# Product one of a seven-product block is copied into a kept PSUM bank, and product two is added onto it by TensorE

## The chip, the cores and the metric

The kernel runs on one core of one Trainium2 chip. The metric is the device time of one execution in microseconds (us). Before the change three runs took 914.67, 915.05 and 915.2 us, so the median is 915.05 us.

## The reference

The reference is a trunk of two layers over one sequence of 256 tokens with 1024 features, all in float32. Each layer has a feed-forward part, a mixer and a second feed-forward part, and each part is followed by a layer norm over a scaled residual:

```python
def swiglu(x, w_in, w_out):
    gu = x @ w_in
    g, u = gu[..., :D_FF], gu[..., D_FF:]
    return (jax.nn.silu(g) * u) @ w_out
...
        x = layer_norm(ALPHA * x + 0.5 * swiglu(x, ffn_w_in[l, 0], ffn_w_out[l, 0]), ln_g[l, 0], ln_b[l, 0])
...
        x = layer_norm(ALPHA * x + y, ln_g[l, 1], ln_b[l, 1])
        x = layer_norm(ALPHA * x + 0.5 * swiglu(x, ffn_w_in[l, 1], ffn_w_out[l, 1]), ln_g[l, 2], ln_b[l, 2])
```

`y` is the mixer's output: a bidirectional mLSTM in the first layer, windowed attention with grouped queries in the second. `D_FF` is 2816. In the kernel this makes six stages: FFN, mLSTM, FFN, FFN, attention, FFN. The change touches the code of the four FFN stages alone, but the order of the work changes in all six.

## The kernel before

Every large product is made in a split form. An operand is written as a high part and a low part in a reduced format, and `mm3` (line 625) does three matmuls for one: high by high, high by low, low by high. A weight tile of 128x1024 is loaded by a DMA into a raw buffer (`w_raw`, `s_raw`). ScalarE casts it to `w_hi` and VectorE subtracts to get `w_lo`. There are ten buffers for each of these two.

An FFN stage works through its 2816 hidden columns in five parts (`PARTS`): two blocks of seven products, a unit, and two more blocks of seven products. A unit is a plain gate and up product for 256 columns. A block, `seven` (line 883), makes 512 hidden columns for two halves of 128 tokens by a Strassen-like scheme: seven products of 128 tokens by 512 columns over half the depth take the place of eight. Some weights of these products are sums of weight tiles. They are formed in the raw buffers, by VectorE (`s_raw<-s_raw,s_raw`) or by a DMA from GpSimd's queue that adds onto a raw buffer. So such a raw buffer is used, added onto, cast again, and used again.

The seven products of a block follow one another in the order 1, 2, 5, 6, 7, 3, 4 of the functions that run behind them: `end1`, `end2`, `end5`, `end6`, `end7`, `end3`, `end4`. Each product is twelve matmuls of 128x512 into one PSUM bank. `qa` takes product one, and later takes others that are added onto what it holds. `qc` takes product two, and `qb` takes product five and later product three. The gate of the first token half is product one plus product two. Before the change `end1` copies `qa` to a buffer `t` in SBUF (ScalarE, `COPY t<-p`), `end2` adds `qc` to it (VectorE, `TENSOR_TENSOR t<-t,p`), and `end6` applies silu in place (ScalarE, `ACTIVATE t<-t`). `end3` is the last to read `qb`. Between the products stand transposes of earlier results (`p<-ident,t`, with `ident` the identity) and pieces of the output product (`down`), whose four banks stay in use through the stage. There are eight PSUM banks in all, shown as `p_88` to `p_95` in the order of the instructions.

What sets the order of all work is a list of numbers. Nothing is issued while the program is described. Every call on an engine is recorded (line 327), and `issue` (line 308) replays the records in the order of the list `ORDER`. A second list, `SLOTS`, says which buffer each request for a tile gets, PSUM banks included. So all instructions on engines and queues carry the line 317 of `issue` in the profile, and they are told apart by their tiles. Each engine takes its own instructions strictly in that order, and waits on semaphores for what it needs from another.

Of the kernel before, what the change touches and what calls it, by code (L numbers as in the profile page):

```python
# [11 lines left out]
AF = mybir.ActivationFunctionType  # L12
# [252 lines left out]
        "365018925167"),  # L265
    "t.0": ("10423251205145435305135232350"),
    "stats": ("101001110110"),
    "mv": ("011010011101"),
    "rs": ("100011011011"),
    "raw.1": ("12301301302312032103102130302130"),  # L270
    "wt.1": ("3210"),
# [1215 lines left out]
```

## Time and profile before

| | before |
|---|---|
| median of three runs | 915.05 us |
| profiled execution, span | 914.3 us |
| PE matmuls | 903.8 us busy, 99%, 4382 of them |
| PE weight loads (PEld) | 748.2 us, 82% |
| VectorE (DVE) | 812.8 us, 89%, 987 instructions |
| ScalarE (ACT) | 576.8 us, 63%, 796 instructions |
| GpSimd (POOL) | 156.8 us, 17% |
| granted TensorE clock | 0.998 |
| memory traffic | 208.52 MB, mean 228 GB/s |

The span of the profiled execution is the time from the first to the last instruction in its trace. It lies 0.75 us below the median of the timed runs. The busy share of an engine is an average over the whole program. PE's share counts a matmul from its start to its end, and successive matmuls overlap, so that a short loss between two of them shows in their start times and not in the share.

### The profile page before, as it was taken

How to read it: one execution, taken by the hardware profiler on the slowest of the kernel's cores; microseconds unless marked ns; L12 is line 12 of the kernel's file. 1: busy time of each engine (PE TensorE's matmuls, PEld its weight loads, DVE VectorE, ACT ScalarE, POOL GpSimd, SP SyncE). 2: the span in 40 equal slices, each digit the busy share in tenths (PEclk: the TensorE clock that was granted, in tenths of full speed). 3: DMA queues.
4: the chain of work that ended last, by engine and by line, in shares of the span. 5: the costliest groups of instructions: out<-in, count | busy, mean ns of one | idle time of the engine just before them, and what ended most of it. 6: DMA issues, size and time to landing. Idle time of an engine off the chain costs nothing.

```text
span 914.3 us, 12376 instructions
## 1 busy us (share of the span) xinstructions
PE 903.8 (99%) x4382; PEld 748.2 (82%) x4382; DVE 812.8 (89%) x987; ACT 576.8 (63%) x796; POOL 156.8 (17%) x200
## 2 busy tenths in 40 slices
PE   9999999999999999999999999999999999999996
PEld 7888888889988888887888888888887788888885
DVE  6998989997798999888999988899899899988897
ACT  6667567557655677565747666666488557666560
POOL 0211112113311121111012111120435311202110
PEclk9999999999999999999999999999999999999999
DMA  9999889558273889898957899987543396997971
GB/s 334 299 298 298 246 248 240 180 179 263 94 260 114 270 252 256 269 280 197 341 196 188 229 277 296 277 178 259 173 173 116 116 277 166 257 303 174 321 182 46
DMA packets 100670, 208.52 MB, mean 228 GB/s; under 512 B 6872, under 2 KB 21232, under 8 KB 100608
## 3 DMA queue, kind: packets, MB, share of 16 engines
q1 hardware_dynamic: 82832, 173.83, 54.1%
q0 software_dynamic: 17632, 33.64, 22.4%
q8 instruction: 34, 0.56, 0.2%
q10 hardware_dynamic: 144, 0.26, 0.1%
q14 instruction: 28, 0.23, 0.1%
HBM read 206.65 MB, written 1.05 MB: 227 GB/s over the span
## 4 chain that ended last, share of the span: by engine, by line
PE 96%; DMA 2%; DVE 1%; issue 1%; ACT 0%; DVEq 0%; POOL 0%; POOLq 0%
PE p L317 96%; DMA s_raw<-in_ffn_w_in_dram 1%; DMA ln_g<-in_ln_g_dram 1%; DVE w_lo L317 0%; DVE x L317 0%; ACT w_hi L317 0%; DVE h_lor L317 0%; DVEq L1483 0%; DVE hc_lor L317 0%; DVE t L317 0%; ACT xT_hi L317 0%; DVE stats L317 0%; DVE mv L317 0%; POOL ji L317 0%; DVE ident L317 0%
## 5 line engine op out<-in xcount | busy, mean ns | idle before, releaser
L317 ACT CAST w_hi<-s_raw 128x1024 fp32r<-128x1024 f32 x239 | 244.5, 1051 | 94.5 <-PE p L317 56.4
L317 DVE TENSOR_TENSOR w_lo<-s_raw,w_hi 128x1024 fp32r<-128x1024 f32 x239 | 285.6, 1218 | 19.6 <-ACT w_hi L317 15.6
L317 ACT CAST w_hi<-w_raw 128x1024 fp32r<-128x1024 f32 (+1 forms) x167 | 172.1, 1041 | 77.9 <-PE p L317 37.6
L317 DVE TENSOR_TENSOR w_lo<-w_raw,w_hi 128x1024 fp32r<-128x1024 f32 (+1 forms) x167 | 199.8, 1208 | 14.5 <-ACT w_hi L317 13.3
L317 PE MATMUL p<-w_hi,xT_hi 128*128 128x512 f32 x512 | 191.9, 394 | 0.8 <-ACT w_hi L317 0.5
L317 PE MATMUL p<-w_lo,xT_hi 128*128 128x512 f32 x512 | 192.1, 394 | 0.0
L317 PE MATMUL p<-w_hi,xT_lo 128*128 128x512 f32 x512 | 191.3, 394 | 0.0
L317 PE MATMUL p<-w_hi,h_lor 128*128 128x512 f32 (+1 forms) x323 | 119.9, 390 | 0.1
L317 PE MATMUL p<-w_hi,h_hir 128*128 128x512 f32 (+1 forms) x323 | 119.5, 391 | 0.0
L317 PE MATMUL p<-w_lo,h_hir 128*128 128x512 f32 (+1 forms) x323 | 118.6, 389 | 0.0
L317 PEld LDWEIGHTS p<-w_hi,xT_hi 128*128 128x128 f32 x512 | 95.8, 188 | 20.4 <-ACT w_hi L317 1.0
L317 PEld LDWEIGHTS p<-w_lo,xT_hi 128*128 128x128 f32 x512 | 96.0, 188 | 19.5 <-DVE w_lo L317 0.4
L317 PEld LDWEIGHTS p<-w_hi,xT_lo 128*128 128x128 f32 x512 | 96.1, 188 | 19.3 <-DVE xT_lo L317 0.3
L317 POOL DMA_DIRECT2D s_raw<-in_ffn_w_in_dram x43 | 52.2, 1266 | 329.0 <-DVE w_lo L317 90.5
L317 PE MATMUL p<-w_hi,S_hir 128*128 128x512 f32 x256 | 96.9, 390 | 0.0
L317 PE MATMUL p<-w_hi,S_lor 128*128 128x512 f32 x256 | 96.8, 390 | 0.0
L317 PE MATMUL p<-w_lo,S_hir 128*128 128x512 f32 x256 | 96.8, 390 | 0.0
L317 PEld LDWEIGHTS p<-w_hi,h_lor 128*128 128x128 f32 x323 | 60.6, 188 | 12.6 <-DVE h_lor L317 0.5
L317 PEld LDWEIGHTS p<-w_lo,h_hir 128*128 128x128 f32 x323 | 60.7, 188 | 12.2
L317 PEld LDWEIGHTS p<-w_hi,h_hir 128*128 128x128 f32 x323 | 60.5, 188 | 12.3 <-ACT h_hir L317 0.2
L317 PEld LDWEIGHTS p<-w_hi,S_hir 128*128 128x128 f32 x256 | 48.0, 188 | 10.5 <-ACT t L317 0.4
L317 PEld LDWEIGHTS p<-w_lo,S_hir 128*128 128x128 f32 x256 | 48.1, 188 | 10.1 <-DVE w_lo L317 0.2
(187 smaller groups left out, 1176.7 us busy)
## 6 DMA issues: line engine op xcount, KB each, us to landing
s_raw<-in_ffn_w_in_dram SPq DMA_DIRECT2D x101, 512.0 KB, 6.0
w_raw<-in_ffn_w_in_dram SPq DMA_DIRECT2D x58, 512.0 KB, 6.3
s_raw<-in_ffn_w_out_dram SPq DMA_DIRECT2D x55, 512.0 KB, 5.8
s_raw<-in_ffn_w_in_dram POOLq DMA_DIRECT2D x43, 512.0 KB, 7.1
w_raw<-in_ffn_w_out_dram SPq DMA_DIRECT2D x33, 512.0 KB, 7.1
w_raw<-in_ml_w_in_dram SPq DMA_DIRECT2D x24, 512.0 KB, 5.2
w_raw<-in_ffn_w_in_dram POOLq DMA_DIRECT2D x21, 512.0 KB, 7.8
s_raw<-in_ffn_w_in_dram SPq DMA_DIRECT2D x20, 256.0 KB, 6.1
```

The source lines that it names most:

```text
L317: f(*args, **kw)
```

## The change

In the second, third and fourth block of every FFN stage `qc` is no fresh bank. It is the bank `qb` of the block before, which is kept from there (`kept`). In these twelve blocks `end1` is a ScalarE copy from the bank `qa` into the kept bank. Product two starts without clearing the bank (`not seed` is the start flag, and it stands for the flag `onto` too), so TensorE adds it onto the copied product one. `end2` then applies silu straight from the bank. The addition on VectorE is gone there. In the first block of a stage nothing is kept, and the copy and the addition remain. Silu moves from `end6` to `end2` in all sixteen blocks.

```diff
+            kept = []
+
             def seven(downs, turns):
...
-                qa, qc = wbank(), wbank()
+                qa = wbank()
+                qc = kept.pop() if kept else None
+                seed = qc is not None
+                qc = qc if seed else wbank()
 
                 def end1():
-                    v["g0"] = copied(qa, "e1")
+                    if seed:
+                        nc.scalar.copy(qc, qa)
+                    else:
+                        v["g0"] = copied(qa, "e1")
 
                 def end2():
-                    nc.vector.tensor_add(v["g0"], v["g0"], qc)
+                    if seed:
+                        v["g0"] = temp("g0")
+                        nc.scalar.activation(v["g0"], qc, AF.Silu)
+                    else:
+                        nc.vector.tensor_add(v["g0"], v["g0"], qc)
+                        nc.scalar.activation(v["g0"], v["g0"], AF.Silu)
...
                 def end6():
                     v["u0"] = copied(qa, "e2")
-                    nc.scalar.activation(v["g0"], v["g0"], AF.Silu)
...
                 product(qa, of(0, 0), True, end1)
                 for f in turns:
                     f()
-                product(qc, of(4, 0), True, end2)
+                product(qc, of(4, 0), not seed, end2)
                 down(downs[0])
                 qb = wbank()
+                kept.append(qb)
```

The lists `ORDER` and `SLOTS` are new throughout. The first line of `ORDER`, out of 218 before and 197 after:

```diff
-    "0 10 -9 8 2 -9 11 -10 11 15 1 -26 11 1 -11 12 1 -12 13 12 -24 13 1 11 -10 1 1 1 1 1 8 -7 17 -37 28 10 1 72 "
...
+    "0 10 -9 8 2 1 -10 11 1 1 -12 13 392 -391 1 394 -393 -12 13 1 1 -18 1 406 -405 113 -111 15 384 -383 1 112 "
...
```

The number of matmuls is 4382 before and after, with the same shapes. VectorE has 12 instructions of 128x512 fewer. ScalarE has as many as before: 12 copies go to a bank and no longer to SBUF, and 12 of 16 silus read a bank and no longer SBUF. The loads are the same.

Three places show how the new lists move the work. The first is PE around products one and two of the second block of the first stage. Before, product one goes to `p_92` and product two to `p_88`; the matmuls of both are mixed with each other, with pieces of the output product (right operand `h_...`) and with product five (`S_...`):

```order
L317 MATMUL p_92<-w_lo_83,xT_hi 128x512
L317 MATMUL p_95<-ident,t_5_157 128x128 x4
L317 MATMUL p_88<-w_lo_85,xT_hi 128x512
L317 MATMUL p_91<-w_hi_69,S_hir_0_158 128x512
L317 MATMUL p_93<-w_lo_78,h_hir_1_99 128x512
L317 MATMUL p_88<-w_hi_76,xT_lo 128x512
L317 MATMUL p_92<-w_hi_70,xT_lo 128x512
L317 MATMUL p_88<-w_hi_76,xT_hi 128x512
L317 MATMUL p_90<-w_hi_71,h_hir_1_99 128x512
```

After, product one goes to `p_93` and product two to the kept bank `p_94`:

```order
L276 MATMUL p_93<-w_lo_85,xT_hi 128x512
L276 MATMUL p_93<-w_hi_75,xT_lo 128x512
L276 MATMUL p_89<-ident,t_3_155 128x128 x4
L276 MATMUL p_91<-w_hi_76,h_hir_1_99 128x512
L276 MATMUL p_91<-w_lo_86,h_hir_1_99 128x512
L276 MATMUL p_91<-w_hi_76,h_lor_1_101 128x512
L276 MATMUL p_90<-w_hi_76,h_hir_1_99 128x512
L276 MATMUL p_94<-w_hi_77,xT_hi 128x512
L276 MATMUL p_94<-w_lo_87,xT_hi 128x512
```

Product two now begins only behind the last matmul of product one, with four transposes and four other matmuls between them. In the twelve blocks there are always four transposes there, and beside them two other matmuls of 128x512 once, three four times, four six times and five once.

The second place is ScalarE at the same block. Before, the copy of product one stands among casts of weights, and the silu of its sum follows thirteen rows later:

```order
L317 CAST h_hir_1_99<-p_95 128x4x128
L317 CAST w_hi_70<-s_raw_6_108 128x1024
L317 COPY t_5_157<-p_92 128x512
L317 CAST w_hi_74<-w_raw_65 128x1024
L317 CAST w_hi_69<-s_raw_7_109 128x1024
```

After, the copy goes into the kept bank:

```order
L276 ACTIVATE t_2_154<-p_92 128x512
L276 CAST w_hi_68<-s_raw_7_109 128x1024
L276 COPY p_94<-p_93 128x512
L276 CAST h_hir_1_99<-p_89 128x4x128
L276 CAST w_hi_70<-w_raw_65 128x1024
```

The cast right ahead of the copy needs a raw buffer onto which VectorE has added another. In nine of the twelve blocks the instruction ahead of the copy is such a cast; in two it is a cast of a buffer that was only loaded, and in one a cast that waits for neither.

The third place is PE in the attention stage, where the scores are made (left operand `kk`, 64 rows; right operand `q2r`). Before, six such matmuls stand together, and other products separate them from the next six:

```order
L317 MATMUL p_90<-kk_hir_0_227,q2r_0_238 128x256
L317 MATMUL p_91<-kk_hir_0_227,q2r_0_238 128x256
L317 MATMUL p_92<-xT_hi,w_hi_71 128x256
L317 MATMUL p_94<-xT_hi,w_lo_83 128x256
L317 MATMUL p_92<-xT_lo,w_hi_71 128x256
...
L317 MATMUL p_92<-xT_lo,w_hi_76 128x256
L317 MATMUL p_90<-kk_hir_0_227,q2r_0_238 128x256
L317 MATMUL p_90<-kk_lor_0_228,q2r_0_238 128x256
```

After, twelve stand together:

```order
L276 MATMUL p_89<-xT_lo,w_hi_74 128x256
L276 MATMUL p_89<-xT_hi,w_lo_78 128x256
L276 MATMUL p_90<-kk_hir_0_227,q2r_0_238 128x256
L276 MATMUL p_91<-kk_hir_0_227,q2r_0_238 128x256
L276 MATMUL p_90<-kk_lor_0_228,q2r_0_238 128x256
...
L276 MATMUL p_91<-kk_hir_0_227,q2r_0_238 128x256
L276 MATMUL p_93<-xT_hi,w_hi_77 128x256
```

The 96 score matmuls stood in 18 such groups and now stand in 12. Over the whole program PE changed between kinds of matmul (512 columns, transposes, 256 columns, scores) so that there were 396 runs of one kind, and there are now 203.

More of the change, by code (lines that the diff above doesn't have):

```diff
@@ L39 @@
 ORDER = (
[208 rows of a table removed]
[187 rows of a table added]
 )
 SLOTS = {
-    "raw.0": ("210375894260ab315798a1b2380476593806142893750a61b4735a0286b12a940280"),
-    "p": ("3015273416371651624740737037743003470071732475045321703262751465120457615023462034756305172461503713"
-        "6442055504252022042555024574651034561742340220420324423044423643153426021762340152301647420765314722"
-        "060227602276670206205326743621306753342132312243113214236"),
-    "h_hir.0": ("01001"),
-    "h_lor.0": ("10101"),
-    "w_hi": ("1536089427819056375820935612483172106249564780132954061782549302675180974325916874210359678241306597"
-        "8240637195824063718459026378591430268719546372150862437689061249085367241903758623104975268413908217"
-        "5469870321659748031256784901375628147093568273041695371208346897520134659782013465920871649356809217"
-        "5368049215063874921506387491206537891234706592318672398160257386541934670253891457260389415762058963"
-        "905268715496"),
@@ L261 @@
-    "w_lo": ("8138121742486951046580796125370164658235182350986541234970895268317504678250734095386210549378012564"
-        "3185206793418250671824930568271469351690561739512805381576130867846245869374921053769842501271093864"
-        "2053149782160345781269073541976208452176048318292137523486914603568274168732498103528769175083257419"
-        "2653801479153869204715368940125739846550169834160253046821795345869732804613859740863742798750286574"
-        "365018925167"),
-    "t.0": ("10423251205145435305135232350"),
@@ L267 @@
[L267 to L271, printed above, removed]
-    "a_hir.1": ("1010"),
-    "a_lor.1": ("0101"),
-    "den.1": ("1000"),
-    "hst.1": ("1111"),
-    "hmv.1": ("0110"),
-    "hrs.1": ("1010"),
-    "h_hir.2": ("0111001001"),
-    "h_lor.2": ("1010110101"),
-    "raw.2": ("8974561237058a96142b96a485712380b57326451983b70a26890ab75124a736b74912386b504896312b50a736271085b4a8"
-        "10954573b16809a2546289310a5b06741329"),
@@ L282 @@
-    "t.2": ("0522403125023501514432433105224023511145331025223353143455"),
-    "sc.4": ("4245315103514231504321"),
-    "raw.4": ("14301534402132530145"),
-    "nm.4": ("22010202"),
-    "sm.4": ("10221202"),
-    "pr0_hir.4": ("00100110"),
-    "pr0_lor.4": ("11101011"),
-    "pr1_hir.4": ("10010010"),
-    "pr1_lor.4": ("11000000"),
-    "o.4": ("00001101"),
+    "raw.0": ("012435869074ab12356ab2180456739a5034678a20519b34679a5b401368ab127408"),
+    "p": ("0123547602456132076151416155161415165413620547162303754162705461270450631274167023541326720651347021"
+        "5161215512161516251634730124657034241432443231343241365721435064713256470132406756023451202677072607"
+        "026762062706273453124607513642623244232624234"),
@@ new lines @@
+    "w_hi": ("0124356789102453678910245367918024356179802435761809432576180943257618940325761894037256180937425681"
+        "0937425681097342568109347265180937426518093472651893074261583907426158390476215394761392457832160947"
+        "5208149365074928136507492186350749218635097428613509742861350974862135074869215304678921504637892150"
+        "4679328150769428513706928543170692584371069258437169025843716923508462791358064729135806247158390624"
+        "715839062471"),
+    "w_lo": ("0123456789013254678901325467908132547069813254670981253467098125346709158234670915826347095182364790"
+        "5182364790512836479051832647095182364709518326470918523640791852364079185264307185264370852940761352"
+        "8409632178053249617805324697180532469718025346971802534697180253694718025369471805623947180562394718"
+        "5023649781503294786510394728651039472856103947285613094728561397408261537498062153749806521798430652"
+        "179843065127"),
@@ L292 @@
+    "t.0": ("02043104543524105203413521405"),
+    "raw.1": ("13032103210132013021031202313021"),
+    "wt.1": ("2031"),
+    "a_lor.1": ("1010"),
+    "raw.2": ("465798031627495ab834075698a3b1249a871630b9245a71264185a7093259a6b1706423b80a142b73680a5978346ba05129"
+        "6ab1840956732ab184263a971b809a547106"),
+    "t.2": ("5123540213154320530414253510441324503142154301524053141524"),
+    "sc.4": ("1240305412034521035412"),
+    "raw.4": ("23405142052301054432"),
     "h_hir.5": ("10101"),
-    "h_lor.5": ("10110"),
@@ L294 @@
-    "raw.5": ("301302356a48159237091238b9ba560b79a208614b557a9328069b1a37a14a542813"),
-    "t.5": ("22311504210332350204153145144"),
+    "raw.5": ("1321030249536a78b10268a7931b0425918b37460129a358b72a8563194b5a71063b"),
+    "t.5": ("41104253141024350452123042150"),
 }
```

393 rows, old and new, of the table ORDER are left out of this document.

## The prediction

> **What bounds the kernel now.** I read the page first: the share of each engine, then the chain that ended last.
>
> ```profile
> span 914.3 us, 12376 instructions
> PE 903.8 (99%) x4382; PEld 748.2 (82%) x4382; DVE 812.8 (89%) x987; ACT 576.8 (63%) x796; POOL 156.8 (17%) x200
> PE 96%; DMA 2%; DVE 1%; issue 1%; ACT 0%; DVEq 0%; POOL 0%; POOLq 0%
> ```
>
> TensorE is busy for 903.8 of 914.3 us and makes 96% of the chain. VectorE, though 89% busy, holds 1% of it. So work taken from VectorE is not time taken from the end; it is worth only what it takes out of PE's losses. The chain in order of time shows where these lie:
>
> ```profile
> 1.71 4.11 PE p L317 x18
> 5.84 0.58 ACT xT_hi L317
> 6.43 0.53 ACT w_hi L317
> 7.00 395.75 PE p L317 x1945
> ...
> 406.25 7.01 DMA s_raw<-in_ffn_w_in_dram
> ...
> 414.50 1.22 DVE w_lo L317
> 415.72 0.60 DVE t L317
> ...
> 416.97 10.74 PE p L317 x49
> ...
> 430.73 232.36 PE p L317 x1065
> ...
> 670.07 236.55 PE p L317 x1186
> 906.62 0.02 issue
> 906.64 0.43 DVE x L317
> ```
>
> PE runs in four long pieces. The start until 7.00 and the tail from 906.64 are chains of their own. Between them the chain leaves PE near 415, 430 and 670. The losses there are read from PE's starts, where two matmuls of 128x512 follow each other at a steady pace:
>
> ```profile
> 322.08 0.39 PE L317 MATMUL p<-w_lo,h_hir 128*128 128x512 f32 x1
> 322.30 0.39 PE L317 MATMUL p<-w_hi,h_lor 128*128 128x512 f32 x1
> ...
> 415.27 0.84 PE L317 MATMUL p<-w_lo,hc_hir 128*128 128x512 f32 x3
> 416.37 0.50 PE L317 MATMUL p<-w_hi,xT_hi 128*128 128x512 f32 x1 [0.26 <-DVE t L317]
> 416.97 0.50 PE L317 MATMUL p<-w_hi,hc_lor 128*128 128x512 f32 x1
> ...
> 430.29 0.39 PE L317 MATMUL p<-w_hi,S_hir 128*128 128x512 f32 x1
> 430.73 0.50 PE L317 MATMUL p<-w_hi,h_lor 128*128 128x512 f32 x1
> 431.07 0.39 PE L317 MATMUL p<-w_hi,h_hir 128*128 128x512 f32 x1
> ```
>
> The pace is 0.22 to 0.23 us from start to start (322.08, 322.30), though one lasts 0.39: its own end comes 0.39 after its start. At 415 the third matmul of the first row starts at 415.27 + 0.84 - 0.39 = 415.72, the next at 416.37 and the next at 416.97. Those two steps are 0.65 and 0.60, so 0.80 us is lost. At 430 two steps of 0.44 and 0.34 lose 0.33. That is **1.1 us** at two places. Everywhere else in the FFN stages PE is dense, as the busy time by stretches shows (the columns after the length are sum or PE, PEld, DVE, ACT, POOL, then clock, DMA share and GB/s):
>
> ```profile
> 10.00:170.00 160.00, 160.00 (x730) 132.08 (x729) 148.10 (x150) 109.56 (x130) 20.51 (x18) 1.00 0.94 277
> 400.00:440.00 40.00, 39.59 (x175) 31.33 (x174) 35.73 (x35) 24.43 (x30) 4.79 (x4) 1.00 0.85 234
> 440.00:640.00 200.00, 200.00 (x915) 164.63 (x914) 183.10 (x195) 127.20 (x153) 25.18 (x21) 1.00 0.84 247
> ```
>
> With PE filled for 160.00 of 160.00 us there is little to win there, and any new wait is a loss.
>
> **The change part by part.** The groups that it touches:
>
> ```profile
> L317 DVE TENSOR_TENSOR t<-t,p x56: 413/679/691, 13.5 to 885.4; 128x512 f32<-128x512 f32 x48, 128x256 f32<-128x256 f32 x8
> L317 ACT COPY t<-p x52: 565/587/595, 8.5 to 880.0; 128x512 f32<-128x512 f32 x52
> L317 ACT ACTIVATE t<-p x32: 371/592/600, 25.6 to 894.9; 128x512 f32<-128x512 f32 x24, 128x256 f32<-128x256 f32 x8
> L317 ACT ACTIVATE t<-t x16: 622/626/637, 50.0 to 880.4; 128x512 f32<-128x512 f32 x16
> ```
>
> *VectorE.* Twelve additions of 0.679 us leave: 12 x 0.679 = 8.1 us of its 812.8. They lie beside PE, so I count 0. The same 1.1 us at 415 and 430 is all they could release, and the list decides that as well; it is counted below, once.
>
> *ScalarE.* Twelve silus read a bank in place of SBUF: 12 x (0.592 - 0.626) = -0.4 us. Twelve copies write a bank in place of SBUF. No row shows a write of ScalarE to a bank. The nearest row is the copy that reads one, 0.587; for a bank at both ends I take the same, with 0.45 and 0.75 as bounds (a quarter either way; at 0.75 only the shortest of the places below would lose, 0.07). ScalarE is 63% busy, so the sum on it is hidden: 0.
>
> *The wait that is new.* Product two must start on a bank that holds product one. After the last matmul of product one starts, that takes 0.39 (its end), 0.59 (copy) and two hand-overs of about 0.03 (the chain's pieces called issue are 0.02 where an engine starts on another's word): 1.04 us. Before, the copy had until the end of product two, and PE never waited for it. The new order puts four transposes and two to five other matmuls in between. Transposes follow at 0.109:
>
> ```profile
> 32.18 0.39 PE L317 MATMUL p<-w_lo,xT_hi 128*128 128x512 f32 x1
> 32.41 0.60 PE L317 MATMUL p<-ident,t 128*128 128x128 f32 x4
> 32.77 0.47 PE L317 MATMUL p<-w_lo,S_hir 128*128 128x512 f32 x1
> 33.08 0.40 PE L317 MATMUL p<-w_hi,xT_lo 128*128 128x512 f32 x1
> ```
>
> From 32.18 to 33.08 four transposes and one matmul pass in 0.90 us. Each further matmul adds 0.227, so the twelve places give 1.13 (once), 1.35 (four times), 1.58 (six) and 1.81 (once). Less 1.04, the slack is 0.09, 0.31, 0.54 and 0.77. A copy that starts on time costs nothing at any of them. But ScalarE takes its queue in order, and in nine places the cast ahead of the copy waits for a raw sum of VectorE:
>
> ```profile
> L317 ACT CAST w_hi<-s_raw 128x1024 fp32r<-128x1024 f32 x239 | 244.5, 1051 | 94.5 <-PE p L317 56.4 <-DVE s_raw L317 17.9 <-DMA s_raw<-in_ffn_w_in_dram 12.2
> ```
>
> Casts take 1.05 us, and ScalarE stood 17.9 us waiting for such sums and 12.2 for loads. If the copy comes late by half a cast (0.53) at all twelve, the loss is 0.44 + 4 x 0.22 = 1.3; by a whole cast it is 0.96 + 4 x 0.74 + 6 x 0.51 + 0.28 = 7.3. On time it is 0. I take **+0.6**, half of the middle case, since before the change PE's waits name ScalarE with one wait in the whole program:
>
> ```profile
> PE p L317 <- ACT w_hi L317: 0.5, 1, 0.5
> ```
>
> The Trainium skill has a rule on the copy. Its page "ScalarE: Activation LUTs", section "Step-by-step: what each stage is for", says that ScalarE reaches PSUM sooner than SBUF as a destination, of use only if TensorE does not need most of PSUM. The trace agrees for the source (0.592 against 0.626) and shows no destination; by the rule the copy would fall below 0.587, and the +0.6 would shrink by at most 0.034 x 12 = 0.4 if the destination gave as much as the source. The limit that the rule adds speaks against the change, because all eight banks are in use.
>
> *The kept bank.* One bank is now held from one block to the next, and across the unit. In the new order a bank that has to be read before it is written again has at least nine matmuls of PE in between in the FFN stages; in the old one 33 reuses in the program had under eight. So it costs nothing that the order hasn't paid: 0, and 0.3 for each of the four units (the two short evacuations there, 0.371 and 0.413, come about that much after PE's last matmul) as the other end.
>
> *PE's order elsewhere.* The same matmuls run in 203 runs of a kind, not 396. Around transposes that is nearly nothing: in the rows above four of them and two wide steps take 0.90, where 4 x 0.109 + 2 x 0.227 = 0.89. Around scores it is not:
>
> ```profile
> 703.85 0.40 PE L317 MATMUL p<-pr_lor,v1r 128*128 128x512 f32 x1
> 704.17 0.38 PE L317 MATMUL p<-kk_hir,q2r 64*128 64x256 f32 x1
> 704.48 0.50 PE L317 MATMUL p<-w_lo,q2r 128*128 128x512 f32 x1
> 704.82 0.40 PE L317 MATMUL p<-w_hi,q2r 128*128 128x512 f32 x1
> ```
>
> A lone score matmul stretches three steps to 0.32 + 0.31 + 0.34 = 0.97. Two wide steps and half of a wide one would be 0.57. So entering and leaving a group costs up to 0.40. Six groups fewer: -2.4 at most, and -0.9 if joining them beside transposes or narrow matmuls saves 0.15 each. I take 0.25 each: **-1.5**.
>
> *The two stalls.* The one at 415 began with a load that VectorE waited for, until 413.26 in the chain; the one at 430 with `w_lo` and `h_lor` in VectorE's queue. New lists place both anew. The new order has 12 waits on ScalarE or VectorE with under 1.4 us of PE's own work in front, where the old had 32, so I take both as gone: **-1.1**, the ends being 0 and -1.1.
>
> *Start and tail.* The tail from 906.64 has the same instructions in the same order. At the start casts of weights and of `xT` change places; the first wide matmul came at 7.00, after casts of 0.58 and 0.53, so either cast hidden earns half a microsecond, and a weight that lands late takes it back: 0, from -0.5 to +0.5.
>
> Sum on the profiled execution: 914.3 - 1.1 - 1.5 + 0.6 = 912.3. The median of the runs is 0.75 above that execution's span, so **913.0 us**.
>
> **The rivals.** *No change that can be told* (a measurement of this kernel tells 0.2%, 1.8 us, from nothing): the score groups save the lower 0.9, new stalls take the place of the two old ones, and the copies cost 0.6: 915.05 - 0.9 + 0.6, about 914.8. For it speaks that PE has 99%; against it, the longer distances in the new order.
>
> *Slower: the copies come late.* One mechanism: VectorE's raw sum is late, the cast behind it holds ScalarE's queue, the copy stands behind the cast, and product two holds PE. Each link is in the trace: at 415 PE stood for 0.80 us behind a late load and VectorE. With the copies 0.9 us late at all twelve the loss is 0.81 + 4 x 0.59 + 6 x 0.36 + 0.13 = 5.5, and with the gains of 1.5 and 1.1 the time is 915.05 - 2.6 + 5.5 = 917.9. It decides from about 0.8 us of lateness on (4.3 of loss), where the sum passes 916.9. Against it: VectorE has 8.1 us less to do, and ScalarE a third of its time free.
>
> *Faster still:* no copy is late, the score groups give 2.4 and the start gives 0.5: 914.3 - 1.1 - 2.4 - 0.5 + 0.75 = 911.0. For it speaks that slack exists in all twelve places.
>
> *The change doesn't do what it says*, if product two waited longer than for the copy, or the scheduler put work elsewhere; the order shows the copies and the twelve missing additions, so this gets nothing.
>
> **How the numbers follow.** The forecast (911.9 to 914.0) gets 0.45, no change (914.0 to 916.9) 0.22, slower 0.20, faster still 0.13. Faster by over 0.2% means below 913.2, which takes the last case and 0.31 of the first: 0.44. Slower means above 916.9: 0.20. The rest is 0.36. For 8 in 10 the range goes from 910.8 to 917.2: its low end is the faster rival with a little left out, its high end reaches into the slower one to a lateness of about 0.8. The likeliest case's own range is 911.9 to 914.0.
>
> **What would show it.** The group `t<-t,p` of 128x512 has 36 and a copy from bank to bank 12, near 0.59 us. The steps at 415 and 430 are gone, PE's waits name no copy with more than 0.6 us in total, and the score groups number 12, with the same 0.3 us steps at their edges. I am wrong if PE waits for ScalarE's copies by several microseconds, if the cast ahead of them waits for sums of VectorE, if new steps of over 0.4 us stand elsewhere in PE's starts, or if a joined group of scores saves nothing.

## The result, and the profile after the change

Four runs of the changed kernel took 924.89 to 927.39 us, median 926.77. Four of the kernel before, beside them, took 914.08 to 915.20, median 914.86. The ratio is **1.0124, with a 95% interval of 1.0110 to 1.0139**: slower by about 11 us, where 913.0 was forecast, with a range up to 917.2. The profiled execution of the changed kernel has a span of 924.8 us, 10.5 more than before. Of all executions told of here one, that of `new_lists_old_start_attention` in the profiler, ran at a granted clock of 0.751 and took 1132.79 us; it is in no ratio.

The page of the changed kernel, first the span, then the busy time of the engines, then the groups by shape that the change touches:

```profile
span 924.8 us, 12419 instructions
PE 905.4 (98%) x4382; PEld 748.7 (81%) x4382; DVE 802.3 (87%) x975; ACT 573.8 (62%) x796; POOL 149.3 (16%) x200
L276 DVE TENSOR_TENSOR t<-t,p 128x512 f32<-128x512 f32 x36 | 24.5, 681 | 3.0 <-PE p L276 2.7
L276 ACT COPY t<-p 128x512 f32<-128x512 f32 x40 | 22.2, 587 | 15.7 <-PE p L276 15.4 <-DVE xT_lo L276 0.3
L276 ACT COPY p<-p 128x512 f32<-128x512 f32 x12 | 6.9, 573 | 5.5 <-PE p L276 5.5
```

The edit did what it says. VectorE has twelve additions fewer and is busy 10.5 us less; twelve copies go from bank to bank, at 0.573 us each. PE's own work is as before, and yet the span is longer: PE waits more. Its waits before (what PE waited for, us in total, how often, the longest):

```profile
PE p L317 <- DVE ident L317: 1.7, 1, 1.7
PE p L317 <- ACT w_hi L317: 0.5, 1, 0.5
PE p L317 <- DVE t L317: 0.3, 1, 0.3
```

and the eight largest in the changed kernel:

```profile
PE p L276 <- DVE nm L276: 2.2, 4, 0.7
PE p L276 <- DVE o L276: 2.1, 2, 1.2
PE p L276 <- DVE ident L276: 1.7, 1, 1.7
PE p L276 <- ACT t L276: 1.3, 2, 1.1
PE p L276 <- DVE w_lo L276: 1.2, 3, 0.8
PE p L276 <- ACT w_hi L276: 1.1, 2, 0.6
PE p L276 <- ACT h_hir L276: 0.7, 1, 0.7
PE p L276 <- ACT p L276: 0.5, 2, 0.3
```

The three waits of before are 2.5 us in all. Now there are ten kinds, 11.4 us in all, most of them small. The copies (`ACT p`) are 0.5 us of them. The two largest, `nm` and `o`, belong to the attention stage, where the edit changed nothing.

To place the loss I took the steps of PE from the start of one matmul to the start of the next, in both traces. For each sequence of kinds (the matmul before, this one and the next: 512 columns, 256, 258, transpose, score) the median step is taken as what PE needs. What a step has above it is loss, and what it has below it is taken off:

| stretch of PE's matmuls | loss before, us | loss after, us |
|---|---|---|
| start (first 60) | 3.2 | 5.0 |
| first FFN | 0.3 | 2.9 |
| mLSTM | 0.5 | 0.9 |
| second FFN | 2.0 | 1.7 |
| third FFN | 0.5 | 2.8 |
| attention | 0.0 | 5.7 |
| fourth FFN | 0.3 | 0.7 |
| sum | 6.9 | 19.7 |
| sum of the medians | 897.4 | 895.3 |

PE needs 2.1 us less in the new order, 1.9 of it in the attention stage. It loses 12.8 more: 5.7 in attention, 5.3 in the four FFN stages and the mLSTM together, 1.8 at the start.

How such a stall comes about shows around 623 us, in the third FFN stage. The rows are those of GpSimd, then ScalarE, then PE (start, duration, and in brackets the idle time before it and what ended it):

```profile
609.13 2.44 POOL L276 DMA_DIRECT2D w_raw<-in_ffn_w_in_dram  x2 [5.59 <-DVE w_lo L276]
...
621.94 1.05 ACT L276 CAST w_hi<-w_raw 128x1024 fp32r<-128x1024 f32 x1 [4.03 <-DMA w_raw<-in_ffn_w_in_dram]
622.89 1.07 ACT L276 COPY t<-p 128x512 f32<-128x512 f32 x2
...
623.52 0.50 PE L276 MATMUL p<-w_hi,S_hir 128*128 128x512 f32 x1 [1.06 <-ACT t L276]
```

Two loads that add onto a raw buffer are issued at 609.13. The cast that needs one waits 4.03 us for it. Behind that cast, in ScalarE's queue, stand two copies that have nothing to do with the load, and PE waits 1.06 us for them. PE's wait is named after the copy; the load is what is late. This load, the second of the two, took 11.6 us from its issue to its landing, the longest of the 64 that add onto a raw buffer.

### The profile page after: what moved, and what is told of

Same layout as the page of the kernel before. It is cut to its first block, busy times and chain, and to the rows that moved or that the text cites. A ratio compares the mean times of both kernels' runs of the same rounds, so it can differ in the third digit from the quotient of the medians.

```text
span 924.8 us, 12419 instructions
## 1 busy us (share of the span) xinstructions
PE 905.4 (98%) x4382; PEld 748.7 (81%) x4382; DVE 802.3 (87%) x975; ACT 573.8 (62%) x796; POOL 149.3 (16%) x200
## 5 line engine op out<-in xcount | busy, mean ns | idle before, releaser
L276 DVE TENSOR_TENSOR w_lo<-s_raw,w_hi 128x1024 fp32r<-128x1024 f32 x230 | 274.6, 1220 | 29.7 <-ACT w_hi L276 29.0
L276 ACT CAST w_hi<-s_raw 128x1024 fp32r<-128x1024 f32 x230 | 234.3, 1052 | 102.0 <-DVE s_raw L276 50.6
L276 DVE TENSOR_TENSOR w_lo<-w_raw,w_hi 128x1024 fp32r<-128x1024 f32 (+1 forms) x176 | 210.6, 1207 | 29.8 <-ACT w_hi L276 26.2
L276 ACT CAST w_hi<-w_raw 128x1024 fp32r<-128x1024 f32 (+1 forms) x176 | 180.3, 1041 | 79.7 <-PE p L276 25.3
L276 PE MATMUL p<-w_hi,xT_hi 128*128 128x512 f32 x512 | 203.3, 398 | 2.1 <-ACT w_hi L276 1.1
L276 PE MATMUL p<-w_lo,xT_hi 128*128 128x512 f32 x512 | 199.8, 391 | 0.5 <-DVE w_lo L276 0.4
L276 PE MATMUL p<-w_hi,xT_lo 128*128 128x512 f32 x512 | 199.4, 391 | 0.0
L276 PE MATMUL p<-w_hi,h_hir 128*128 128x512 f32 (+1 forms) x323 | 126.0, 393 | 0.7 <-ACT h_hir L276 0.7
L276 PE MATMUL p<-w_lo,h_hir 128*128 128x512 f32 (+1 forms) x323 | 125.1, 388 | 0.8 <-DVE w_lo L276 0.8
L276 PEld LDWEIGHTS p<-w_hi,h_hir 128*128 128x128 f32 x323 | 60.6, 188 | 13.1 <-ACT h_hir L276 1.5
L276 PEld LDWEIGHTS p<-w_hi,h_lor 128*128 128x128 f32 x323 | 60.7, 188 | 12.8 <-DVE h_lor L276 0.6
L276 PEld LDWEIGHTS p<-w_hi,S_lor 128*128 128x128 f32 x256 | 48.0, 188 | 10.0
```

The source lines that it names most:

```text
L276: f(*args, **kw)
```

## The experiments

**The new lists without the copies, and the copies in the old lists.** The first two kernels part the edit from the lists. `new_lists_add` keeps the new lists and undoes the edit:

```diff
-                    if seed:
-                        nc.scalar.copy(qc, qa)
-                    else:
-                        v["g0"] = copied(qa, "e1")
+                    v["g0"] = copied(qa, "e1")
...
+                    nc.vector.tensor_add(v["g0"], v["g0"], qc)
+                    nc.scalar.activation(v["g0"], v["g0"], AF.Silu)
...
-                product(qc, of(4, 0), not seed, end2)
+                product(qc, of(4, 0), True, end2)
```

> The new lists are kept, and the change in the blocks is undone: in all blocks ScalarE copies product one to SBUF, product two clears its bank, and VectorE adds (12 additions of 0.68 us more, put right ahead of their silu). Theory A, the new lists cost the time and not the copies: 925 to 928 us, within 1.5 of the changed kernel's 926.8, and the attention stage keeps its waits on VectorE's nm and o (4.3 us in the trace of the changed kernel). Theory B, the copies into the kept bank and what is queued behind them cost it: 915 to 919 us.

Measured: 930.62 us (926.35 to 931.79), ratio to before 1.0152 (1.0125 to 1.0180). That is far from theory B and above A's own 925 to 928 us, so the new lists cost the time. Without the copies they are as slow, perhaps slower: the intervals of 1.0152 and 1.0124 overlap, so whether the copies save 2 to 3 us there stays unclear. In this trace PE waits 3.9 us for VectorE's `t`, where the changed kernel has 0.2.

`old_lists_copy` makes the edit in the kernel before, and moves only what has to move:

```diff
+                seed = kept[0]
+                kept[0] = True
...
+                    if seed:
+                        nc.scalar.copy(qc, qa)
+                    else:
+                        v["g0"] = copied(qa, "e1")
...
-                product(qc, of(4, 0), True, end2)
+                product(qc, of(4, 0), not seed, end2)
```

> The old lists are kept, and the blocks are changed alone: in twelve blocks ScalarE copies product one into the (fresh) bank of product two, product two is moved behind the copy with at least eight matmuls between it and product one, silu reads the bank, and the 12 additions go. What doesn't hang on it stays in the old order. Theory A, the lists cost the time: 914 to 917 us, PE waiting under 2 us for the copies. Theory B, the copies cost it: 920 to 928 us.

Measured: 928.70 us, ratio 1.0146 (1.0129 to 1.0163). This is theory B's time, and it seemed to contradict the first run. But the kernel carries two things, the copies and a moved product two. (Its sums also seem to lack part of product one in two blocks, which the last section takes up.) One of its stalls is the slower rival of the prediction, link by link (VectorE, ScalarE, PE):

```profile
66.95 1.22 DVE L314 TENSOR_TENSOR s_raw<-s_raw,s_raw 128x1024 f32<-128x1024 f32 x1
...
68.29 1.05 ACT L314 CAST w_hi<-s_raw 128x1024 fp32r<-128x1024 f32 x1 [2.14 <-DVE s_raw L314]
69.24 0.58 ACT L314 COPY p<-p 128x512 f32<-128x512 f32 x1
...
69.87 0.50 PE L314 MATMUL p<-w_hi,xT_hi 128*128 128x512 f32 x1 [1.01 <-ACT p L314]
```

A raw sum is late, the cast waits for it, the copy stands behind the cast, and product two waits 1.01 us. Over the program PE waited 1.9 us for copies here, three times, while its loss by starts is 12.4 us more than before.

`old_lists_moved` therefore takes the very order of `old_lists_copy` and puts the old operations back (copy to SBUF, addition, silu in place):

```diff
-                    if seed:
-                        nc.scalar.copy(qc, qa)
-                    else:
-                        v["g0"] = copied(qa, "e1")
+                    v["g0"] = copied(qa, "e1")
...
-                product(qc, of(4, 0), not seed, end2)
+                product(qc, of(4, 0), True, end2)
```

> The order of the run old_lists_copy without the copy: product two stands behind product one as there, but ScalarE copies product one to SBUF, VectorE adds and silu works in place, as before the change. If the copy into the bank is what costs (PE waits until ScalarE, which takes its queue in order, has reached it), the time falls back to 914 to 918 us. If holding product two back is what costs (its weights, their casts and the raw sums behind them all move, in a list that had no room for it), it stays at 924 to 930 us, near the 928.7 of old_lists_copy.

Measured: 925.92 us, ratio 1.0103 (1.0087 to 1.0118). It stays slow with no copy into a bank at all. Most of the 12 us of `old_lists_copy` is the moved order; the copies add 0.43% or about 4 us there (1.0146 against 1.0103, intervals that don't touch), of which the two traces show 1.5. Moved in this way, product two costs some 9 us: it goes back by up to 72 places in a list of over 6600, twelve times, and other entries with it. Another way of moving it was not tried.

**The attention stage.** Here the new list puts twelve score matmuls together. `new_lists_old_attention` returns this stretch to the old order. Only the lists change, so there is no diff of code.

> The changed kernel, with the stretch from the first score matmul to the last use of q2r in the old order and the old buffers (377 matmuls of PE); the rest as in the changed kernel, save for buffers that had to be chosen otherwise at the seams. The traces give 65.7 us for this stretch in the changed kernel and 61.9 before. If the twelve score matmuls that now stand together are what stalls (their second half writes banks that VectorE still reads), the time falls by 3 to 5 us, to 922 to 924 us, and the waits on nm and o go from 4.3 us to under 1. If the stretch is only late because of what came before it (loads, VectorE's queue), it stays at 925 to 928 us.

Measured: 926.71 us, ratio 1.0125 (1.0099 to 1.0151), so no gain. (The expectation counts the stretch 1.2 to 1.3 us longer at its ends than the times by PE's starts below.) But the waits on `nm` had become one of 4.1 us, right at the seam, the place where one order gives way to the other: a cast on ScalarE waited 2.7 us there for a late load of attention weights, and VectorE, due to read the first scores, stood behind that cast. `new_lists_old_attention_2` moves the seam forward:

> As new_lists_old_attention, with the seam 220 matmuls of PE earlier, so that the loads of the attention weights come in the old order too; in the first try one seam stall of 4.3 us (VectorE waited for such a load ahead of the first scores) hid the effect. If the joined score groups are the cause of the 5.8 us lost in that stage, its stalls on nm and o are gone, the time is 921 to 924.5 us. If a stretch in the old order still loses over 4 us in the attention stage without a seam stall, the cause lies in front of it.

Measured: 928.17 us, ratio 1.0124 (1.0109 to 1.0139). Again no gain in time, and again for a seam stall of 4.2 us, now before the stage. ScalarE's row and PE's:

```profile
636.77 1.04 ACT L276 CAST w_hi<-w_raw 128x1024 fp32r<-128x1024 f32 x1 [4.51 <-DMA w_raw<-in_at_w_in_dram]
637.72 0.58 ACT L276 CAST h_hir<-p 128x512 fp32r<-128x512 f32 x1
...
638.35 0.80 PE L276 MATMUL p<-w_hi,h_hir 128*128 128x512 f32 x1 [4.20 <-ACT h_hir L276]
```

The clock fell at this seam too (columns as in the next view; 0.50 and 1.00 are the granted clock):

```profile
637.70:644.50 6.80, 6.15 (x15) 4.79 (x16) 5.83 (x6) 1.55 (x3) 0.00 (x0) 0.50 0.17 40
644.50:660.00 15.50, 15.50 (x75) 12.75 (x74) 12.07 (x16) 4.78 (x6) 4.78 (x7) 1.00 0.47 165
```

For 6.8 us the steps of 128x512 matmuls were 0.43 us in place of 0.23, which by the medians costs 3.0 us on top of the stall. The first try lost 2.3 us in the same way.

Behind this seam, however, the stage itself is whole. The same kernel from the first score matmul to the last use of `q2r` (length, then busy time of PE, PEld, DVE, ACT and POOL, granted clock, DMA share and GB/s):

```profile
682.70:744.00 61.30, 61.28 (x384) 48.08 (x383) 54.43 (x131) 46.25 (x122) 29.15 (x56) 1.00 0.34 113
```

PE is filled for 61.28 of 61.30 us. By PE's starts the stretch from the first score to the last `q2r` takes 60.6 us, as it did before, against 64.5 in the changed kernel. So the loss of the attention stage is in the new list's order of that stage, and not brought in from ahead of it. The whole time of these two kernels tells nothing: the stage alone won 3.9 us in the second, and the seam, its stall and the low clock together, lost 6.5 us in the first and 7.4 in the second. `new_scores_closed_up` has no seam. It moves 45 places of the changed kernel's list:

> The changed kernel with one thing moved in the attention stage: in four of the eight pairs of score banks a read by VectorE stood in the list between the matmuls of one bank, so that PE had to wait for it; there the second six matmuls now stand right behind the first six. If these reads are what holds PE (four waits on nm, 2.2 us in the trace), 1 to 2.5 us are gained and nm's waits fall under 0.8 us. If VectorE is simply behind there, the wait turns up on the transposes or on o and the time stays within 0.8 us.

Measured: 923.76 us, ratio 1.0084 (1.0065 to 1.0102), against 1.0124 of the changed kernel. PE at the second pair of banks, in the changed kernel:

```profile
683.86 0.40 PE L276 MATMUL p<-kk_hir,q2r 64*128 64x256 f32 x4
684.09 0.28 PE L276 MATMUL p<-kk_lor,q2r 64*128 64x256 f32 x1
684.85 0.38 PE L276 MATMUL p<-kk_lor,q2r 64*128 64x256 f32 x1 [0.48 <-DVE nm L276]
```

and with the six closed up:

```profile
683.29 0.40 PE L276 MATMUL p<-kk_hir,q2r 64*128 64x256 f32 x4
683.53 0.28 PE L276 MATMUL p<-kk_lor,q2r 64*128 64x256 f32 x2
683.65 0.28 PE L276 MATMUL p<-kk_hir,q2r 64*128 64x256 f32 x2
...
PE p L276 <- DVE o L276: 2.1, 2, 1.2
PE p L276 <- DVE nm L276: 0.4, 1, 0.4
```

The waits on `nm` fall from 2.2 to 0.4 us. In the trace the stage from first score to last `q2r` goes from 64.5 to 62.9; the 2.1 us on `o` stay. Reads by VectorE that the new list put between the matmuls of one bank held PE. The runs show more gain (0.4%, some 3.5 us, but with intervals of 0.15% to 0.2% either way) than the 1.6 us of the trace, whose execution (925.05 us) was the slowest of its four; what the rest is stays open.

**The loads that are added onto raw buffers.** `new_lists_no_added_loads` leaves out one term of the weight sums:

```diff
-                nc.gpsimd.dma_start(t.rearrange("p (k f) -> p k f", k=self.words[w]["k"]), v, accum_op=OP.add)
+                pass
```

> The changed kernel without the 64 loads that add onto a raw buffer (33.6 MB), so one term of the weight sums is left out. If the stalls in the FFN stages (some 6 us more than before, two of them seen behind a cast that waited for such a load) come from these loads being late, the time falls by 4 to 7 us, to 920 to 923 us, with the attention stage as slow as it was. If they come from ScalarE's and VectorE's order alone it stays above 925 us.

Measured: 922.43 us, ratio 1.0074 (1.0056 to 1.0093), 0.5% or 4.6 us under the changed kernel. The loss in the FFN stages and the mLSTM falls from 9.0 to 3.7 us, what it was before the change; attention (5.8) and start (5.1) stay. The control does the same in the kernel before:

> The kernel before without the 64 loads that add onto a raw buffer (one term of the weight sums is left out), as a control of new_lists_no_added_loads, which was 4.3 us faster than the changed kernel. If the old lists leave these loads time enough, it gains only what its own two stalls hold, 0 to 2 us: 913 to 916 us beside the kernel before. If these loads are a burden of 4 us in any order, it gains 3 to 5 us.

Measured: 914.51 us, ratio 0.9982 (0.9972 to 0.9992). The old list gains 1.6 us, about what its stalls at 415 and 430 held. So these loads are no burden of 4 us in themselves; the new order gives them too little time. `new_small_added_loads` keeps the loads and all their waits, and cuts the bytes:

```diff
-                nc.gpsimd.dma_start(t.rearrange("p (k f) -> p k f", k=self.words[w]["k"]), v, accum_op=OP.add)
+                nc.gpsimd.dma_start(t.rearrange("p (k f) -> p k f", k=self.words[w]["k"])[:, :, 0:64], v[:, :, 0:64], accum_op=OP.add)
```

> The changed kernel with the 64 added loads cut to 64 of 512 columns (the rest of that term of the weight sums is left out); their issue, their place in every queue and all waits stay. If the transfer of these loads is what comes late, the time falls like without them, by 3 to 5 us, to 921.5 to 924 us. If it is GpSimd's queue and the chain of waits, it stays within 1.5 us of the changed kernel.

Measured: 923.27 us, ratio 1.0078 (1.0063 to 1.0093). It is the transfer and not GpSimd's queue. How ScalarE's casts waited, in the changed kernel:

```profile
L276 ACT CAST w_hi<-s_raw 128x1024 fp32r<-128x1024 f32 x230 | 234.3, 1052 | 102.0 <-DVE s_raw L276 50.6 <-PE p L276 25.5 <-DMA s_raw<-in_ffn_w_in_dram 19.8
L276 ACT CAST w_hi<-w_raw 128x1024 fp32r<-128x1024 f32 x172 | 177.9, 1051 | 75.1 <-PE p L276 25.3 <-DVE w_raw L276 25.0 <-DMA w_raw<-in_ffn_w_in_dram 15.2
s_raw<-in_ffn_w_in_dram POOLq DMA_DIRECT2D x43, 512.0 KB, 7.4
w_raw<-in_ffn_w_in_dram POOLq DMA_DIRECT2D x21, 512.0 KB, 8.6
```

and with the small loads:

```profile
L276 ACT CAST w_hi<-s_raw 128x1024 fp32r<-128x1024 f32 x230 | 234.1, 1054 | 81.9 <-DVE s_raw L276 49.7 <-PE p L276 24.7 <-issue 2.0
L276 ACT CAST w_hi<-w_raw 128x1024 fp32r<-128x1024 f32 x172 | 178.3, 1052 | 64.8 <-PE p L276 26.2 <-DVE w_raw L276 24.9 <-DMA w_raw<-in_ml_w_in_dram 7.0
```

The waits on VectorE's sums, the largest entry by far (17.9 us before the change), are the same in both (50.6 and 49.7). The waits on loads, 19.8 and 15.2 us, are gone, and PE's loss in the FFN stages and the mLSTM falls from 9.0 to 4.2 us, near the 3.7 of before: so what is left of the waits on sums costs PE little. Matching the 64 added loads of both traces with their first users gives the reason: from issue to first use a load had a median of 11.1 us before, with 23 of 64 under 10 us, and has 9.6 us now, with 36 under 10. Landing takes as long as before, a median of 7.6 us in both. So in 25 cases now, and 12 before, the cast starts within 0.15 us of the landing: the load is what it waited for.

**The copy's own room.** `new_copy_twice` makes each copy into the kept bank twice:

```diff
                         nc.scalar.copy(qc, qa)
+                        nc.scalar.copy(qc, qa)
```

> The changed kernel with each of the twelve copies into the kept bank made twice, one right behind the other (0.57 us each in its trace). By the slack counted in the prediction (0.09, four times 0.31, six times 0.54, 0.77) copies that start on time would cost 0.48 + 4 x 0.26 + 6 x 0.03 = 1.7 us more: 927.5 to 929.5 us. If the copies are late already and PE waits for each, all of it shows: 12 x 0.57 = 6.8 us, 932 to 935 us. If they have far more room than counted, under 1 us.

Measured: 929.14 us, ratio 1.0139 (1.0121 to 1.0157), 0.15% or 1.4 us above the changed kernel's, inside the interval of both. PE's waits for copies rise from 0.5 us to this:

```profile
PE p L277 <- ACT p L277: 2.0, 5, 0.6
```

That is 1.5 us more, where the slack that was counted gives 1.7; PE's whole loss by starts is 0.9 us more. This fits copies that start on time in the new list and have the room that was counted, and it rules out that PE waits for every copy already, which would have added 6.8 us.

**The start.** `new_lists_old_start` and, with the attention stage too, `new_lists_old_start_attention` put PE's first 100 matmuls into the old order; again only lists change.

> The changed kernel with PE's first 100 matmuls and all that goes with them in the old order. Its trace lost 5.0 us in the first 60 matmuls, that of before 3.2. If the start of the new list is at fault, 1 to 2.5 us are gained: 924 to 926 us. If the loads are merely shifted, the loss turns up behind the seam and the time is 926 to 929 us.

Measured: 931.21 us, ratio 1.0164 (1.0147 to 1.0182). The first 60 matmuls lose 3.8 us in place of 5.0, but a new stall follows behind the seam, and behind it another 1.8 us at a granted clock of 0.50:

```profile
PE p L265 <- DVE t L265: 6.2, 1, 6.2
```

> As new_lists_old_attention_2, and PE's first 100 matmuls with all that goes with them in the old order too. The start (first 60 matmuls) lost 5.0 us in the changed kernel's trace and 3.2 before. If the start's loss is the list's, this kernel is another 1 to 2.5 us faster than new_lists_old_attention_2: 919 to 923 us. What is then left over the kernel before (4 to 8 us) lies in the FFN stages alone.

Measured: 931.17 us, ratio 1.0157 (1.0140 to 1.0174), with no trace to set beside the others. The start's order accounts for about 1.2 of the 1.8 us by the trace of `new_lists_old_start`; as a gain in time that is not shown, since that kernel loses more at its seam. The start also varies by itself: in the seven other traces that keep the new start, the first 60 matmuls lose 5.1 to 7.0 us, in the three that keep the old one 3.1 to 3.5.

## Why the prediction was wrong

**What was right.** The bound: PE's matmuls are 98% of the span, and twelve additions less on VectorE bought nothing. The copy: 0.573 us, where 0.587 was taken. Its rule from the Trainium skill ("ScalarE: Activation LUTs", "Step-by-step: what each stage is for"), that PSUM is the nearer destination, points the right way, and is worth 14 ns a copy here. The new wait: 0.6 us was taken and PE waited 0.5 us for copies; the number was half of a middle case, so that it fits this closely is luck, but the slack behind it fits `new_copy_twice`. PE's order: -1.5 was taken, and the medians give -2.1.

**The step that failed: "I take both as gone".** The part on the two stalls counted waits on ScalarE or VectorE with under 1.4 us of PE's own work in front (12 in place of 32), and concluded that the old stalls go and none come. The count measures how far a wait is from the matmul that releases it. A stall that begins with a load, as the one at 415 did, has no such matmul, so it isn't in the count. The runs showed that these are the ones that matter in the FFN stages: the added loads have less time from issue to use, and without their transfers 4 to 5 us are gone. The term was set to -1.1 and came out at about +5 for the FFN stages and the mLSTM. One of the prediction's own signs of being wrong came true here: new steps of over 0.4 us elsewhere in PE's starts (the largest in the FFN stages loses 1.2 us at 622.08).

**What was not looked at: the attention stage's banks.** The price of a joined group was taken from its edges alone. For banks the prediction said that a reuse has at least nine matmuls in between in the FFN stages, and counted that as the answer. In the attention stage the new order has five places with three or fewer, and the old order none under seven. The stage's new order saved 1.9 us of steps and cost 5.7 of stalls. Of these, 1.8 us (`nm`) went when four pairs were closed up; for the 2.1 us on `o` and the rest no run shows which part of the order is at fault.

**The start** was put at 0, from -0.5 to +0.5, with the reason that a hidden cast and a late weight cancel. It lost 1.8 us more. This term was mis-sized.

**The rivals.** The slower one was on the right side and its chain, a late sum or load, then a cast, then what stands behind it in ScalarE's queue, is what the trace shows. But it was tied to the twelve copies and priced by their slack. Any instruction behind a late cast does the same (`t`, `h_hir`, `w_hi`), and there are many more of these. That kept its time at 917.9. (Its sum at 0.8 us of lateness is 916.7, not yet the 916.9 that it names; that takes a little more.) All cases, the range too, were built on one list being as good as the other but for the places named. The order showed that every place of the list had changed, and no case had the price of that: `old_lists_moved` puts it at 1% for a list of which far less was moved.

**What stays open:** whether the copies save time in the new list (1.0124 against 1.0152, with overlapping intervals), what makes up the difference between the 1.6 us in the trace and the 0.4% in the runs of the closed-up scores, what holds PE on `o`, and how much of the start's loss is the list's. A list that serves the copies and has neither the late loads nor the split banks was not tried. No kernel tried here beats the one before with its work whole.

## What to carry to other kernels

When a change comes with a new schedule, price the schedule first: check, for each queue that an engine takes in order, how long every load has from issue to first use, and how far apart the uses of every bank are, in all stages and not only the edited one. The largest wait of an engine need not be the costly one (50 us of waits on sums cost little here, 35 us on loads cost about 5), so test a suspected wait by taking its cause away. And a part of one schedule set into another makes seams, whose stalls, and the low clock behind them, can be larger than the effect looked for; a local move within one schedule is the cleaner test.

## What was not expected of the hardware

**A low clock behind a long wait.** In three kernels (`new_lists_old_attention`, `new_lists_old_attention_2`, `new_lists_old_start`) PE waited 4.1, 4.2 and 6.2 us at a seam. Each time the granted clock fell to 0.50 within the wait and stayed there for 6.8 us, which cost 2.3, 3.0 and 1.8 us behind the stall. In the other traces set side by side here no wait of PE after the first 30 us is over 1.35 us, and from there on the clock stays at 1.00 until PE's work is done. Near its start, though, `new_lists_add` has 0.50 for 3.4 us behind waits of 1.1 and 0.5 us. What it takes in general, no run here shows.

**A sum onto a copy.** Whether TensorE adds onto what ScalarE put into a bank seems to hang on what TensorE itself wrote there before. In `old_lists_copy` the copy goes into a fresh bank. In two of its twelve blocks TensorE had last written transposes of 128 columns each into that bank, and the output is off by 0.057 of the reference; in the changed kernel TensorE's last write to the kept bank was always a whole product. That the transposes are what breaks the sum, so that part of product one is missing, is argued from the order of the instructions, and was not tried by itself. It agrees with what the Trainium skill's page "PSUM — Partial Sum Buffer", section "The four PSUM rules", says of the hidden bits that only TensorE sets and clears, and it may be why the change keeps `qb`'s bank. The advice of the same page of the Trainium skill, section "Summary: rules for kernel authors", that a bank filled by ScalarE must hold zero is stricter than what these runs show: in the changed kernel a copy that is not zero is added onto.
